# The scan's table placed between the two sums of values, and its old bank given to transposes

## The chip, the cores and the metric

The kernel runs on one core of a Trainium2 chip. The metric is the device time of one execution in microseconds (us). Three runs of the kernel before gave 1956.85, 1957.84 and 1957.93 us; the median is 1957.84 us.

A core has a matrix engine (PE; its weight loads are shown apart as PEld), a vector engine (DVE), a scalar engine (ACT), a third elementwise engine (POOL) and a queue that issues transfers (SP). Each takes its instructions in order, and semaphores order one engine's work against another's. Results of the matrix engine go to PSUM, a memory of 128 partitions with eight banks of 512 float32 values each; DVE and ACT read it there.

## The reference, cut to what matters

One decoder layer is computed on 1024 tokens of width 1024, with 16 learned meta tokens ahead of them. In order: a half-weighted SwiGLU, a normalisation and one joint projection, two groups of heads side by side (four HGRN2 heads and eight stick-breaking attention heads), an output projection, and a second SwiGLU. The change touches the stick-breaking attention alone:

```python
def block(args):
    qblk, start = args
    qpos = start + jnp.arange(BLOCK, dtype=jnp.int32)
    z = jnp.einsum('bhqd,bhkd->bhqk', qblk, k) * scale
    allowed = (kpos[None, :] < qpos[:, None]) & valid[None, :]
    log_beta = jnp.where(allowed, jax.nn.log_sigmoid(z), -jnp.inf)
    log_keep = jnp.where(allowed, jax.nn.log_sigmoid(-z), 0.0)
    suffix = lax.cumsum(log_keep, axis=3, reverse=True) - log_keep
    w = jnp.exp(log_beta + suffix)
    return jnp.einsum('bhqk,bhkd->bhqd', w, v)
```

For each block of 128 queries, every key gets a score z. Its weight is sigmoid(z) times the product of sigmoid(-z) over all later allowed keys. The values are summed with these weights.

## The kernel before, in words

**Where the stage lies.** The layer's first SwiGLU and the projections come first; the stick-breaking attention runs from about 860 to 1136 us of the span; the HGRN2 heads, the output projection and the second SwiGLU follow. On the matrix engine the order is the program's own: it is written out by hand (`manual_schedule` for the tensor engine). A planner orders the other engines' instructions and places the semaphore waits that the use of tiles asks for. It goes by the order in which the program emits the instructions: an access that has to be kept apart from an earlier one waits for the earlier one.

**Jobs.** `sb_jobs` makes 32 jobs: eight heads, each with four jobs of two neighbouring query blocks, starting at blocks 0, 6, 2 and 4. A job has three lists of steps.

- `score` (`sb_scores`): a query block's keys are cut into pieces of at most 512. The function `piece` issues two matmuls into a bank `z` (L1640, L1641), sigmoid(-z) into `keep` and sigmoid(z) into `sig` on ACT (L1642, L1643), and a running product over the reversed keys on DVE (L1646, a scan). The scan's second operand is the table `begin`, in PSUM: zeros with a reversed identity, which starts each row's product at its own diagonal. The piece with the last keys reads as many of its columns as the piece has keys (144 to 457); every other piece reads only its first column, broadcast. After a block's last piece POOL multiplies `sig` by the shifted `keep` (L1653). There are 14 pieces for a head and 112 in all.
- `turn` (`unit`, `meta`, `flip`): the matrix engine transposes the weights, up to four squares of 128 into one bank (`flip`, L1495, and L1549 for the meta tokens), and `sb_parts` takes them out as a rounded part on ACT (L1618) and a remainder on DVE (L1619), called `wu` and `wm`.
- `value` (`values`): for each block of keys two matmuls (L1570, L1572) add to the job's sum `oacc`, 128 by 256. A job has 3, 9, 5 or 7 such pairs, 24 for a head and 192 in all. After the last, `sb_out` takes the sum out on ACT (L1611) and DVE (L1612).

`braid` lays the jobs over each other: in slot n it issues the scores of job n, the transposes of job n-2 and the values of job n-3, and between them projections for the HGRN2 heads (`proj`, L249 to L251), which need neither. Within a slot the steps are sorted by their place in their list.

**The eight banks during this stage.** Two for scores (`z`), two for transposes (tag `tr`, used in turn), two for sums of values (tag `o`, used in turn), one for the projections, and one, the other projection bank, for the table `begin`. `begin` is written once, just before the braid (L2180, L2181), and only read after that.

Of the kernel before, what the change touches and what calls it, by code (L numbers as in the profile page):

```python
# [11 lines left out]
F32 = mybir.dt.float32  # L12
# [5 lines left out]
PSUM = bass.MemoryType.PSUM  # L18
DRAM = bass.MemoryType.DRAM

P = 128
# [3 lines left out]
META = 16  # L25
# [23 lines left out]
class Block:  # L49
# [1401 lines left out]
    def sb_qk(self, p, qT, kT, pool, mix, dst):  # L1451
# [31 lines left out]
        for src, c0, b0, nb in rows:  # L1483
# [5 lines left out]
                self.put_split(to, p, slice(c0, c0 + n), t[:, :n], mix, gain)  # L1489
            yield 0, 1500  # L1490

    def flip(self, src, spans):
        ps = self.ptr.tile([P, len(spans), P], F32, tag="tr", name="flip")
        for j, (s0, m) in enumerate(spans):
            self.nc.tensor.transpose(ps[:m, j, :], src[:, s0 : s0 + m], self.ident)  # L1495
        return ps

    def sb_jobs(self, keys, fetch, pool):


        nc = self.nc
        qD, kD, vD, oD = keys
        pools = pool
        heads = [(p, hh) for p in range(4) for hh in range(2)]
        kept = {}

        def load(p, hh):
            rows = slice(64 * hh, 64 * hh + 64)
            qs = fetch.tile([P, SEQ], F32R, tag="qs", name="qs", bufs=2)
            ks = [fetch.tile([P, T], F32R, tag=f"ks{i}", name="ks", bufs=2) for i in range(2)]  # L1510
            for i in range(2):
                part = slice(64 * i, 64 * i + 64)
                nc.sync.dma_start(qs.bitcast(F32)[part], qD[p, rows, i])
                for j in range(2):
                    nc.sync.dma_start(ks[j].bitcast(F32)[part], kD[p, rows, j])
            return qs, ks

        def load_v(p, hh):
            v = fetch.tile([P, 9, P], F32R, tag="v", name="v", bufs=2)
            src = vD[p, hh].rearrange("r (j a) c -> r j a c", a=4)  # L1520
            for a in range(4):
                nc.sync.dma_start(
                    v.bitcast(F32)[32 * a : 32 * a + 32],
                    src[:, :, a],
                )
            return v

        def job(p, hh, qs, ks, v, b0):
            sigs, acc, wm, wu = [], [], [], []
            score, turn, value = [], [], []  # L1530
            for bi in range(2):
                score += self.sb_scores(pool, qs, ks, b0 + bi, sigs)

            def unit(u, bi):
                if bi == 0 or b0 == 4 * u - 1:
                    wu.append([
                        pool.tile([P, 4, 256], F32R, tag=f"wu{i}", name="wu", bufs=3)
                        for i in range(2)
                    ])
                spans = [(META + P * j, P) for j in range(4 * u, min(4 * u + 4, b0 + bi + 1))]  # L1540
                ps = self.flip(sigs[bi], spans)
                self.sb_parts([t[:, : len(spans), bi * P : (bi + 1) * P] for t in wu[u]], ps)

            def meta():
                wm.extend(kept["wm"][0])
                kept["wm"].reverse()
                ps = self.ptr.tile([META, 2, P], F32, tag="tr", name="flip")
                for bi in range(2):
                    nc.tensor.transpose(ps[:, bi, :], sigs[bi][:, :META], self.ident)  # L1549
                self.sb_parts([t[:META] for t in wm], ps)  # L1550

            for bi in range(2):
                for u in range(-(-(b0 + bi + 1) // 4)):
                    n = min(4, b0 + bi + 1 - 4 * u)
                    turn.append((107 * n, lambda u=u, bi=bi: unit(u, bi)))
            turn.append((214, meta))

            def values(j):
                if j == 0:
                    acc.append(self.po.tile([P, 256], F32, tag="o", name="oacc"))  # L1560
                o = acc[0]
                if j == b0 + 2:
                    w = [t.rearrange("p b t -> p (b t)") for t in wm]
                    vj, c = v[:, 0], slice(0, 256)
                else:
                    c = slice(128, 256) if j == b0 + 1 else slice(0, 256)
                    w = [t[:, j % 4, c] for t in wu[j // 4]]
                    vj = v[:, 1 + j]
                end = j == b0 + 2
                nc.tensor.matmul(o[:, c], vj, w[0], start=j == 0, stop=False,  # L1570
                                 skip_group_check=True)
                nc.tensor.matmul(o[:64, c], vj[:, :64], w[1], start=False, stop=end,  # L1572
                                 skip_group_check=True)
                if end:
                    self.sb_out(p, hh, b0, o, kept, pool, oD)

            for j in range(b0 + 3):
                value.append((240, lambda j=j: values(j)))
            return score, turn, value

        kept["wm"] = [[fetch.tile([P, 2, P], F32R, name=f"wm{j}{i}") for i in range(2)]
                      for j in range(2)]
        for t in chain(*kept["wm"]):
            nc.vector.memset(t.bitcast(F32), 0.0)
        none = kept["wm"][1][1].rearrange("p b t -> p (b t)").bitcast(F32)[META:]
        for p in range(4):
            for a in range(4):
                to = vD[p, :, 0 if a else META :, a].rearrange("h r c -> r h c")
                nc.sync.dma_start(
                    to, none[: to.shape[0]].rearrange("r (h c) -> r h c", h=2)  # L1590
                )
        ahead, v = load(*heads[0]), load_v(0, 0)
        yield None
        pool = pools[0]
        for i, (p, hh) in enumerate(heads):
            qs, ks = ahead
            if i:
                v = load_v(p, hh)
            for b0 in (0, 6, 2, 4):
                if b0 == 2 and i + 1 < len(heads):  # L1600
                    ahead = load(*heads[i + 1])
                yield job(p, hh, qs, ks, v, b0)
# [171 lines left out]
    def run(self):  # L1774
# [21 lines left out]
        with ExitStack() as c0:  # L1796
            with ExitStack() as c1:
# [8 lines left out]
                with tc.manual_schedule(engines={nc.tensor.engine}), ExitStack() as c2:  # L1806
# [88 lines left out]
                    begin, finish = self.meta_in(marks)  # L1895
# [247 lines left out]
                def after_early():  # L2143
                    pe_ctx.close()
                    self.pz = self.pool("pz", 2, PSUM, c1)
                    self.ptr = self.pool("ptr", 2, PSUM, c1)
                    self.po = self.pool("po", 2, PSUM, c1)

                self.after_early = after_early
                columns = self.hgrn_fill(xh, xl, pst, hgD)  # L2150
# [16 lines left out]
                with tc.manual_schedule(engines={nc.tensor.engine}):  # L2167
# [7 lines left out]
                    with ExitStack() as c2:  # L2175
                        self.att.append(self.pool("att1", ctx=c2))
                        tag = self.proj_tags[0]
                        self.proj_tags = [self.proj_tags[1]] * 2
                        self.begin = self.pproj.tile([P, 512], F32, tag=tag, name="begin", bufs=1)
                        nc.vector.memset(self.begin, 0.0)  # L2180
                        nc.vector.tensor_copy(self.begin[:, 1 : P + 1], self.ident[:, ::-1])  # L2181
                        self.braid(jobs, islice(columns, 76), 1.22, 2.0, 3.0)
                    cf.close()
                    self.proj_tags[0] = tag
                    hg_ctx = ExitStack()
                    hg = self.pool("hg", ctx=hg_ctx, side="right")
# [205 lines left out]
```

## Time and profile before

| what | value |
| --- | --- |
| median of three runs | 1957.84 us |
| the profiled execution's own time | 1959.65 us |
| its span, first to last instruction | 1957.9 us |
| granted matrix clock, mean | 0.999 |
| matrix engine busy in the span | 1919.8 us (98%) |
| vector engine busy | 1390.4 us (71%) |
| scalar engine busy | 849.6 us (43%) |

A busy time is the union of an engine's instructions. The ends of matmuls are modelled, and neighbouring ones overlap in the records, so their spacing tells more than their length. Each row of a timeline gives the start, the length, the engine, the line and the tiles written and read; a bracket gives the idle time of the engine ahead of it and what ended it.

### The profile page before, as it was taken

The numbers are of one execution on the slowest core, as the hardware profiler recorded it, in microseconds if no ns is written. First come the engines' busy times: TensorE is split into PE (matmuls) and PEld (weight loads), VectorE is DVE, ScalarE is ACT, GpSimd is POOL, SyncE is SP. The second block draws the span as 40 slices with busy tenths as digits, with TensorE's granted clock in tenths as the row PEclk, the third lists the DMA queues.
The fourth block names the chain that finished last, engine by engine and source line by source line (L and its number), as shares of the span: only waits on it lengthen the run. The fifth ranks groups of instructions, "written<-read, shape, count | busy, mean of one in ns | idle before, by whom it ended". The sixth has DMA issues, their size and how long they took to land.

```text
span 1957.9 us, 30218 instructions
## 1 busy us (share of the span) xinstructions
PE 1919.8 (98%) x10607; PEld 1616.6 (83%) x10607; DVE 1390.4 (71%) x2184; ACT 849.6 (43%) x1711; POOL 450.5 (23%) x625
## 2 busy tenths in 40 slices
PE   7999999999999999999999999999999999999999
PEld 6888888788888888888898978887888888888887
DVE  7977877877678665467777766677567767766774
ACT  6523443334444544356666635433232332344443
POOL 3010100001000003133333332210544645530000
PEclk9999999999999999999999999999999999999999
DMA  7356887758965315865454177655634444469473
GB/s 213 93 165 170 253 272 243 233 203 291 375 221 188 127 54 144 193 170 148 128 148 121 57 253 225 161 208 183 198 115 140 128 131 121 132 243 318 154 231 113
DMA packets 381687, 355.54 MB, mean 182 GB/s; under 512 B 129040, under 2 KB 284560, under 8 KB 381536
## 3 DMA queue, kind: packets, MB, share of 16 engines
q1 hardware_dynamic: 359728, 288.98, 48.7%
q0 software_dynamic: 20768, 64.63, 9.5%
q8 instruction: 84, 1.38, 0.3%
q14 instruction: 67, 0.55, 0.1%
q10 hardware_dynamic: 1040, 0.00, 0.0%
HBM read 237.95 MB, written 115.57 MB: 181 GB/s over the span
## 4 chain that ended last, share of the span: by engine, by line
PE 89%; DVE 4%; DMA 3%; ACT 2%; issue 1%; POOL 1%; SPq 1%; DVEq 0%; ACTq 0%; POOLq 0%
PE o L732 21%; PE qb L450 18%; PE qa L450 12%; PE qc L450 12%; PE proj L249 5%; PE proj L251 4%; PE proj L250 4%; PE flip L1495 2%; PE wo L250 1%; PE wo L249 1%; PE wo L251 1%; PE mq L1001 1%; PE oacc L1572 1%; PE oacc L1570 1%; DMA oT<-oD 1%
## 5 line engine op out<-in xcount | busy, mean ns | idle before, releaser
L450 PE MATMUL qb<-T,wh 128*128 128x512 f32 x1056 | 344.6, 390 | 1.3 <-ACT T L309 0.8
L450 PEld LDWEIGHTS qb<-T,wh 128*128 128x128 f32 x1056 | 198.1, 188 | 46.4 <-issue 2.5
L450 PE MATMUL qa<-B,wh 128*128 128x512 f32 x696 | 226.7, 390 | 0.3 <-ACT B L835 0.2
L249 PE MATMUL proj<-xh,wh 128*128 128x512 f32 (+2 forms) x640 | 213.2, 333 | 2.6 <-ACT st L1142 1.3
L732 PE MATMUL o<-t,w 128*128 128x512 f32 x924 | 211.8, 390 | 0.7 <-DVE u L543 0.7
L251 PE MATMUL proj<-xl,wh 128*128 128x512 f32 (+2 forms) x640 | 210.2, 328 | 0.8 <-DVE xl L1957 0.8
L250 PE MATMUL proj<-xh,wl 128*128 128x512 f32 (+2 forms) x640 | 210.1, 328 | 0.0
L732 PE MATMUL o<-parts 128*128 128x512 f32 x924 | 209.6, 389 | 0.0
L450 PE MATMUL qb<-T,wl 128*128 128x512 f32 x528 | 205.5, 389 | 0.0
L732 PEld LDWEIGHTS o<-t,w 128*128 128x128 f32 x924 | 172.8, 188 | 37.8 <-ACT sgm L981 1.1
L732 PEld LDWEIGHTS o<-parts 128*128 128x128 f32 x924 | 173.5, 188 | 36.0
L362 DVE TENSOR_TENSOR wl<-s,wh 128x512 fp32r<-128x512 f32 x160 | 165.6, 1035 | 50.8 <-ACT wh L360 49.9
L360 ACT CAST wh<-s 128x512 fp32r<-128x512 f32 x160 | 99.2, 622 | 188.5 <-PE qb L450 141.1
L450 PEld LDWEIGHTS qa<-B,wh 128*128 128x128 f32 x696 | 130.5, 188 | 28.0 <-DVE B L836 0.5
L360 ACT CAST wh<-raw 128x512 fp32r<-128x512 f32 x120 | 74.4, 621 | 155.8 <-PE qc L450 111.4
L450 PE MATMUL qa<-B,wl 128*128 128x512 f32 x348 | 135.4, 389 | 0.0
L249 PEld LDWEIGHTS proj<-xh,wh 128*128 128x128 f32 x640 | 120.8, 189 | 15.0 <-ACT st L1142 2.2
L251 PEld LDWEIGHTS proj<-xl,wh 128*128 128x128 f32 x640 | 120.7, 189 | 12.3 <-DVE xl L1957 1.2
L250 PEld LDWEIGHTS proj<-xh,wl 128*128 128x128 f32 x640 | 120.8, 189 | 10.1
L450 PE MATMUL qc<-B,wh 128*128 128x512 f32 x352 | 115.1, 390 | 2.3 <-DVE u L543 2.3
L450 PE MATMUL qc<-T,wh 128*128 128x512 f32 x352 | 117.0, 394 | 0.0
L450 PEld LDWEIGHTS qb<-T,wl 128*128 128x128 f32 x528 | 99.1, 188 | 20.2
(393 smaller groups left out, 3819.4 us busy)
## 6 DMA issues: line engine op xcount, KB each, us to landing
raw<-in_ffn_w_in_dram SPq DMA_DIRECT2D x176, 256.0 KB, 4.0
raw<-in_ffn_w_out_dram SPq DMA_DIRECT2D x112, 256.0 KB, 4.5
w2in<-both SPq DMA_DIRECT2D x28, 512.0 KB, 3.4
raw<-in_w_in_dram SPq DMA_DIRECT2D x25, 512.0 KB, 5.2
ks<-kD SPq DMA_DIRECT2D x32, 260.0 KB, 4.8
wout<-both SPq DMA_DIRECT2D x16, 512.0 KB, 3.7
wh<-w2in SPq DMA_DIRECT2D x27, 256.0 KB, 3.1
wl<-w2in SPq DMA_DIRECT2D x27, 256.0 KB, 3.1
```

The costliest lines, as they stand in the source:

```text
L249: nc.tensor.matmul(ps, wh[:, s], xs, start=k == 0, stop=False)
L250: nc.tensor.matmul(ps, wl[:, s], xs, start=False, stop=False)
L251: nc.tensor.matmul(ps, wh[:, s], xl[:, k, c0 : c0 + n], start=False, stop=k == nk - 1)
L360: nc.scalar.copy(hi, src)
L362: self.block_lo = nc.vector.tensor_sub(lo, src, hi.bitcast(F32))
L450: nc.tensor.matmul(ps, a[:, k, :], b[:, k, :], start=start and k == 0 and i == 0, stop=k == 3 and i == 2, skip_group_check=True,)
L732: nc.tensor.matmul(banks[bank][m], y[:, m * P : (m + 1) * P], z, start=start and at == 0 and e == 0, stop=q == nq - 1 and e == 2, skip_gro ...
L1001: nc.tensor.matmul(ps[at : at + 32, :], self.xm[:, 4 * h + k, :], got[i, h][:, k, :], start=h == 0 and k == 0, stop=h == 1 and k == 3, til ...
L1495: self.nc.tensor.transpose(ps[:m, j, :], src[:, s0 : s0 + m], self.ident)
L1570: nc.tensor.matmul(o[:, c], vj, w[0], start=j == 0, stop=False, skip_group_check=True)
L1572: nc.tensor.matmul(o[:64, c], vj[:, :64], w[1], start=False, stop=end, skip_group_check=True)
```

## The change

The two sums and the table become one tile of 1024 columns, which is two banks. The first sum is columns 0 to 255 (the first half of the first bank), the second sum columns 768 to 1023 (the second half of the second bank), and the table columns 256 to 767: its first 256 columns in the first sum's bank, its other 256 in the second sum's. Jobs take the two sums in turn, so those starting at blocks 0 and 2 sum in the first bank, and those at 6 and 4 in the second. The bank that held the table, `tag`, is used by every third transpose: `turn_bank` hands it out once in three calls, and the two banks of tag `tr` in turn otherwise. The pool `po` of the later stages is made after the braid. No instruction is added or taken out.

```diff
+    def turn_bank(self, shape):
+
+        self.turned_in = (self.turned_in + 1) % 3
+        if self.spare and not self.turned_in:
+            return self.pproj.tile(shape, F32, tag=self.spare, name="flip", bufs=1)
+        return self.ptr.tile(shape, F32, tag="tr", name="flip")
+
     def flip(self, src, spans):
-        ps = self.ptr.tile([P, len(spans), P], F32, tag="tr", name="flip")
+        ps = self.turn_bank([P, len(spans), P])
...
             def meta():
                 wm.extend(kept["wm"][0])
                 kept["wm"].reverse()
-                ps = self.ptr.tile([META, 2, P], F32, tag="tr", name="flip")
+                ps = self.turn_bank([META, 2, P])
...
             def values(j):
                 if j == 0:
-                    acc.append(self.po.tile([P, 256], F32, tag="o", name="oacc"))
+                    acc.append(self.sums[0])
+                    self.sums.reverse()
...
                     self.ptr = self.pool("ptr", 2, PSUM, c1)
-                    self.po = self.pool("po", 2, PSUM, c1)
...
-                        self.begin = self.pproj.tile([P, 512], F32, tag=tag, name="begin", bufs=1)
+                        both = self.pool("po", 1, PSUM, c2).tile([P, 1024], F32, name="oacc")
+                        self.sums = [both[:, :256], both[:, 768:]]
+                        self.begin = both[:, 256:768]
+                        self.spare, self.turned_in = tag, 0
                         nc.vector.memset(self.begin, 0.0)
                         nc.vector.tensor_copy(self.begin[:, 1 : P + 1], self.ident[:, ::-1])
                         self.braid(jobs, islice(columns, 76), 1.22, 2.0, 3.0)
                     cf.close()
+                    self.spare = None
+                    self.po = self.pool("po", 2, PSUM, c1)
                     self.proj_tags[0] = tag
```

## The prediction

> **What bounds the kernel now.** I read the page's head first, then the table by stretch, for the stage from 860 to 1140 us in which the changed banks are used.
>
> ```profile
> span 1957.9 us, 30218 instructions
> PE 1919.8 (98%) x10607; PEld 1616.6 (83%) x10607; DVE 1390.4 (71%) x2184; ACT 849.6 (43%) x1711; POOL 450.5 (23%) x625
> ...
> 860.00:1140.00 280.00, 270.99 (x1865) 244.43 (x1864) 205.11 (x356) 181.21 (x464) 98.86 (x141) 0.99 0.44 124
> ```
>
> The columns of the last row are the stretch and its length, then busy time and count of PE, weight loads, DVE, ACT and POOL. PE is busy 270.99 of 280 us, so at most 9.0 us can be gained here, while a wait put into PE's order costs its full length: PE takes its instructions in the written order and has nothing else to do meanwhile. DVE has 75 us free and ACT 99. The waits of PE in the stage, next:
>
> ```profile
> PE flip L1495 <- DVE wu L1619: 3.6, 9, 0.8
> PE z L1640 <- ACT sig L1643: 1.9, 5, 0.5
> PE flip L1495 <- DVE wm L1619: 1.8, 3, 0.6
> ...
> PE flip L1549 <- DVE wu L1619: 0.2, 1, 0.2
> ```
>
> (Columns: total, times, longest.) Transposes wait 5.6 us in all (3.6 + 1.8 + 0.2) for a bank that DVE has not emptied. That is what a third bank can take away.
>
> **The new neighbours.** From the groups by tile:
>
> ```profile
> L1646 DVE TENSOR_TENSOR_SCAN keep<-keep,begin x112: 431/909/1160, 864.1 to 1120.4; 128x144 f32<-128x144 f32 x8, 128x272 f32<-128x272 f32 x8, 128x457 f32<-128x457 f32 x8, 128x455 f32<-128x455 f32 x8
> ...
> L1570 PE MATMUL oacc<-wu,v x160: 220/280/368, 874.0 to 1134.5; 128*128 128x256 f32 x128, 128*128 128x128 f32 x32
> ```
>
> Today the 112 scans read a bank that nobody writes. After the change each reads a bank into which PE sums values. By the layout, all 112 touch the first bank (the short read of column 0 too); those with more than 256 columns, seven pieces of a head's fourteen, also touch the second. Whether PE must then wait is the question on which all hangs. One place in the trace bears on it, where DVE reads the first of several products in one bank (columns: start, length, engine, line, tiles, idle time before):
>
> ```profile
> 1192.87 1.83 PE L1321 MATMUL up<-vr,vT 128*128 128x128 f32 x14
> ...
> 1193.18 0.68 DVE L1257 TENSOR_TENSOR KB<-KB,F 128x512 f32<-128x512 f32 x1
> ...
> 1194.07 0.73 DVE L1324 SCALAR_TENSOR_TENSOR F<-F,Ts,up 128x128 f32<-128x128 f32 x2 [0.20 <-PE up L1321]
> ```
>
> The fourteen matmuls fill two banks, eight then six, at 0.13 us each. DVE needs only the first two, done by about 1193.4, and is free at 1193.86; it still waits 0.20 us for PE, until the eighth is done (1192.87 + 8 x 0.13 = 1193.9, and the pipeline's end). So disjoint columns do not part two engines in this program: the wait covers the bank or the tile. A sum and the table within one bank will be kept apart the same way.
>
> [...]
>
> **Which side waits, and for how long.** Order goes by emission. `piece` emits two z matmuls, two ACT passes and the scan in one go. A values step placed after it must therefore wait for that scan, although PE reaches it within a fraction of a microsecond. A scan's wait for earlier sums is free: PE has passed them before it reaches this piece's z. For `sb_out` the last values step has already waited. A usual place, from the timeline:
>
> ```profile
> 877.59 0.31 PE L1641 MATMUL z<-ks,qs 128*128 128x328 f32 x1
> ...
> 877.74 0.22 PE L1570 MATMUL oacc<-wu,v 128*128 128x128 f32 x1
> ...
> 878.01 0.45 ACT L1642 ACTIVATE keep<-z 128x328 f32<-128x328 f32 x1
> ...
> 878.62 0.89 DVE L1646 TENSOR_TENSOR_SCAN keep<-keep,begin 128x327 f32<-128x327 f32 x1
> ```
>
> The sum's matmul starts 0.15 us after z's second; the scan ends at 879.51. It would be 1.77 us late. Behind it on PE stand the next transposes, z and projections; ACT's `keep` and `wu` passes and DVE's remainders wait for those, so nothing overtakes.
>
> I went so through all 192 value pairs, by job (even jobs first bank, odd jobs second), each against the last scan emitted before it that touches its bank, counting each scan once. 64 pairs come too early. The first and the last:
>
> ```profile
> 873.50 0.32 PE L1641 MATMUL z<-ks,qs 128*128 128x328 f32 x1
> ...
> 874.01 0.36 PE L1570 MATMUL oacc<-wu,v 128*128 128x256 f32 x1
> ...
> 874.20 1.47 DVE L1646 TENSOR_TENSOR_SCAN keep<-keep,begin 128x263 f32<-128x263 f32 x2
> ...
> 1116.30 0.34 PE L1641 MATMUL z<-ks,qs 128*128 128x392 f32 x1
> ...
> 1116.83 0.36 PE L1570 MATMUL oacc<-wm,v 128*128 128x256 f32 x1
> ...
> 1117.54 0.96 DVE L1646 TENSOR_TENSOR_SCAN keep<-keep,begin 128x393 f32<-128x393 f32 x1
> ```
>
> They are 875.67 - 874.01 = 1.66 and 1118.50 - 1116.83 = 1.67 us late. All 64 add up to 109 us: 96 for 46 pairs that follow their piece within 0.55 us, 13 for 18 pairs with projections between. This is the upper bound, since it has today's queues on ACT and DVE. Those get shorter when PE pauses. The lower bound takes for each size the fastest way seen from z to the scan's end:
>
> ```profile
> L1642 ACT ACTIVATE keep<-z 128x264 f32<-128x264 f32 x16 | 6.2, 386 | 4.6 <-PE z L1641 4.6
> ...
> L1642 ACT ACTIVATE keep<-z 128x456 f32<-128x456 f32 x16 | 8.9, 556 | 1.4 <-PE z L1641 0.9
> ...
> L1646 DVE TENSOR_TENSOR_SCAN keep<-keep,begin 128x455 f32<-128x455 f32 x8 | 9.2, 1154 | 0.9 <-ACT keep L1642 0.8
> ...
> L1646 DVE TENSOR_TENSOR_SCAN keep<-keep,begin 128x265 f32<-128x265 f32 x8 | 5.6, 701 | 3.4 <-ACT keep L1642 3.4
> ```
>
> For 264 keys that is 0.28 (z) + 0.39 + 0.70 and two hand-overs of 0.1, or 1.58 us; for 456 it is 0.37 + 0.56 + 1.15 and 0.07, or 2.15. Summed over the 64 it is 84 us. I take **92**, nearer the lower bound, as ACT and DVE will be only about half busy.
>
> **What comes with the waits.** A hand-over from DVE to PE costs time once more:
>
> ```profile
> 901.42 0.39 DVE L1619 TENSOR_TENSOR wm<-flip,wm 16x256 fp32r<-16x256 f32 x1
> ...
> 901.95 0.41 PE L1495 MATMUL flip<-ident,sig 128*128 128x128 f32 x2 [0.58 <-DVE wm L1619]
> ```
>
> DVE ends at 901.81, PE starts 0.14 us later. 64 of them are 0 (if hidden in the weight load) to 9 us; I take **5**. Then the granted clock, from stretches cut at its one drop within the stage (after the length stand the five engines' busy times, then the clock):
>
> ```profile
> 850.21:853.63 3.42, 2.11 (x18) 1.90 (x16) 2.30 (x4) 3.28 (x6) 1.26 (x5) 1.00 0.98 336
> ...
> 863.87:867.28 3.41, 2.39 (x11) 1.46 (x11) 3.17 (x5) 3.14 (x9) 1.30 (x4) 1.00 0.83 230
> 867.28:870.69 3.41, 3.41 (x11) 2.73 (x10) 3.20 (x6) 1.46 (x5) 2.12 (x3) 0.50 1.01 205
> ...
> 869.38 0.63 PE L250 MATMUL proj<-xh,wl 128*128 128x512 f32 x1
> 869.81 0.63 PE L251 MATMUL proj<-xl,wh 128*128 128x512 f32 x1
> ...
> 871.14 0.39 PE L249 MATMUL proj<-xh,wh 128*128 128x512 f32 x1
> 871.37 0.40 PE L250 MATMUL proj<-xh,wl 128*128 128x512 f32 x1
> ```
>
> After a stretch of 3.41 us in which PE paused for 1.0 us, the clock was halved for the next 3.41 us: matmuls of 512 columns came every 0.43 us in place of 0.23. Another stretch with 1.3 us of pause had no such sequel; it has 18 matmuls against 11. At 0.23 us for 512 columns (a transpose's counted twice) the columns streamed fill 41% of the stretch that led to a drop and 52% of the other. With the 64 waits spread over the stage's 1865 matmuls, 11 to 16 stretches (lower bound of the waits) or 19 to 27 (upper) fall under 41 to 47%. A drop costs at most 8 x 0.20 = 1.6 us, less where the stretch also holds waits; say 14 drops at 1.2, rounded to **16** us; bounds 0 and 43.
>
> [...]
>
> **The gain.** The 5.6 us of transpose waits and most of the z waits vanish, since DVE and ACT catch up in every pause: **-7** (bounds 0 and -9, all the idle time of the stage).
>
> **At nothing.** The table is set up where it was, once:
>
> ```profile
> 863.20 0.48 DVE L2180 MEMSET begin<- 128x512 f32 x1
> 863.23 0.48 PE L1640 MATMUL z<-ks,qs 128*128 128x456 f32 x1 [0.33 <-ACT sig L1643]
> ```
>
> PE waits for ACT there, not for the table; an earlier start is worth between 0 and about 1 us. A scan that reads across two banks has no row; the nearest, 457 columns in 1.10 us within one bank, gives 2.4 ns a column and DVE has 75 us free, so 0 with +1 at most. No transfer is issued elsewhere. The pool made after the braid waits for the last `sb_out`, as its banks do today: 0.
>
> **Sum** against the profiled execution's 1959.65 us: 92 + 5 + 16 - 7 = +106, or 2065.7; it lay 1.8 above the median, so **2064 us**. All low ends give 84 - 9 = +75, all high ends 109 + 9 + 43 = +161.
>
> **Rivals.** [...] *Waits by tile, not by bank*: the row at 1194.07 fits both, as its tile is one bank. Then every scan holds up every sum: 92 pairs, 120 to 163 us late; 131 + 7 + 22 - 8 = +152, or 2110 us. *Only the first bank binds*: if long scans are not counted into the second bank, 46 pairs, 57 to 77 us late; 62 + 4 + 10 - 6 = +70, or 2028 us. *The change does only what its words say*: columns do part the engines, no value waits for a scan, and the third bank takes away up to 5.6 us of transpose waits; about 4 gained, 1954 us. This ends on the other side, and decides if the values' rows keep starting 0.15 us after z. Against it speaks the 0.20 us wait at 1194.07, which columns alone would not explain.
>
> **How the numbers follow.** Chances: the forecast 0.55, waits without clock 0.15, by tile 0.08, first bank only 0.10, no waits 0.12. The range 2022 to 2102 holds the first two with their unknowns and most of the first-bank case; about 2 in 10 lie outside. Changes under 0.2% (3.9 us) can hardly be told from none. Only the last case is not slower: 0.06 faster, 0.05 the same; slower 0.89.
>
> **What would show it.** In the changed profile: PE `oacc` L1570 waiting for DVE `keep` L1646 some 64 times with a total near 92 us (right), or absent (wrong); PE's busy share in the stage down from 97% to near 75%; the stage some 105 us longer; several stretches at clock 0.5; transposes' waits for `wu` and `wm` nearly gone. A wait count near 92 would mean by tile, near 46 first bank only. The prediction falls if no value pair waits for a scan.

## The result, and the profile after

The changed kernel takes 2138.73 us at the median of five runs (2137.16 to 2146.01); before it is 1957.84 us (1956.85 to 1958.01). The ratio is 1.0931, with a 95% interval from 1.0913 to 1.0948: 9.3% slower, or 181 us. That is outside the predicted range of 2022 to 2102 us. That sums wait for scans, and that this makes the kernel slower, was as forecast. Which accesses wait for each other, and what the waits cost in clock, was not.

The head of the changed kernel's page, and the stage's row in the table by stretch (the stretch and its length, busy time and count of PE, weight loads, DVE, ACT and POOL, then the granted clock, the DMA share and GB/s):

```profile
span 2135.4 us, 30240 instructions
PE 1969.9 (92%) x10607; PEld 1644.7 (77%) x10607; DVE 1392.9 (65%) x2184; ACT 853.9 (40%) x1711; POOL 449.4 (21%) x625
PEclk9999999999999999989999899999999999999999
860.80:1312.50 451.70, 315.39 (x1851) 268.47 (x1850) 202.67 (x323) 184.68 (x462) 97.70 (x140) 0.92 0.27 76
```

The same row of the kernel before, from the first score to the last sum:

```profile
859.00:1135.50 276.50, 267.49 (x1851) 241.68 (x1850) 201.15 (x325) 180.43 (x462) 97.61 (x140) 0.99 0.44 124
```

The stage grew by 175.2 us, of a span that grew by 177.5; the work is the same. PE idles 136.3 us in place of 9.0, and its mean clock fell to 0.92. The waits of PE in the stage after the change (total, times, longest):

```profile
PE oacc L1578 <- DVE keep L1654: 121.8, 80, 3.1
PE oacc L1578 <- DVE ot L1620: 12.7, 9, 3.1
PE z L1648 <- ACT sig L1651: 1.4, 4, 0.5
```

(L1578 is the former L1570, L1654 the scan, L1620 the read-out of a sum.) The transposes' waits are gone, as forecast. The sums of values wait 89 times, 134.5 us: for scans, and, which no step of the prediction had, for the read-out of the other sum. Two places of the timeline show both kinds:

```profile
900.72 0.42 DVE L1620 TENSOR_TENSOR ot<-oacc,olow 64x256 f32<-64x256 f32 x1
...
901.19 0.41 PE L1578 MATMUL oacc<-wu,v 128*128 128x256 f32 x1 [1.10 <-DVE ot L1620]
...
919.34 0.32 PE L1649 MATMUL z<-ks,qs 128*128 128x348 f32 x1
...
920.44 0.93 DVE L1654 TENSOR_TENSOR_SCAN keep<-keep,oacc 128x347 f32<-128x347 f32 x1
...
921.43 0.38 PE L1578 MATMUL oacc<-wu,v 128*128 128x256 f32 x1 [1.56 <-DVE keep L1654]
```

At 901.19 a job starting at block 2 begins its sum in the first bank and waits until DVE has read the sum in the second bank. At 921.43 a job starting at block 4 begins its sum in the second bank and waits for a scan of 347 columns; that is not the piece with a block's last keys, so it reads one column of the first bank. Neither pair shares a bank; both share the tile. Sorted by layout, 26 of the 80 waits for scans, 39.9 of 121.8 us, are of this kind.

### The profile page after: what moved, and what is told of

Its sections match the earlier page's. It is cut to its first block, busy times and chain, and to the rows that moved or that the text cites. A ratio compares the mean times of both kernels' runs of the same rounds, so it can differ in the third digit from the quotient of the medians.

```text
span 2135.4 us, 30240 instructions
## 1 busy us (share of the span) xinstructions
PE 1969.9 (92%) x10607; PEld 1644.7 (77%) x10607; DVE 1392.9 (65%) x2184; ACT 853.9 (40%) x1711; POOL 449.4 (21%) x625
## 5 line engine op out<-in xcount | busy, mean ns | idle before, releaser
L249 PE MATMUL proj<-xh,wh 128*128 128x512 f32 (+2 forms) x640 | 221.2, 346 | 1.6 <-ACT st L1142 1.3
L250 PE MATMUL proj<-xh,wl 128*128 128x512 f32 (+2 forms) x640 | 218.3, 341 | 0.0
L251 PE MATMUL proj<-xl,wh 128*128 128x512 f32 (+2 forms) x640 | 217.4, 340 | 0.8 <-DVE xl L1965 0.8
L1578 PE MATMUL oacc<-wu,v 128*128 128x256 f32 (+1 forms) x160 | 54.7, 351 | 117.6 <-DVE keep L1654 104.8
L1661 POOL TENSOR_TENSOR sig<-sig,keep 128x144 f32<-128x144 f32 (+3 forms) x64 | 81.0, 1266 | 278.6 <-DVE keep L1654 263.9
L1578 PEld LDWEIGHTS oacc<-wu,v 128*128 128x128 f32 x160 | 31.8, 198 | 139.7 <-DVE keep L1654 123.9
L249 PEld LDWEIGHTS proj<-xh,wh 128*128 128x128 f32 x640 | 127.5, 199 | 13.8 <-ACT st L1142 1.5
L251 PEld LDWEIGHTS proj<-xl,wh 128*128 128x128 f32 x640 | 127.3, 199 | 13.4 <-DVE xl L1965 1.2
L250 PEld LDWEIGHTS proj<-xh,wl 128*128 128x128 f32 x640 | 127.3, 199 | 10.8
```

The costliest lines, as they stand in the source:

```text
L249: nc.tensor.matmul(ps, wh[:, s], xs, start=k == 0, stop=False)
L250: nc.tensor.matmul(ps, wl[:, s], xs, start=False, stop=False)
L251: nc.tensor.matmul(ps, wh[:, s], xl[:, k, c0 : c0 + n], start=False, stop=k == nk - 1)
L1661: nc.gpsimd.tensor_mul(sig, sig, keep[:, 1 : nk + 1])
```

## The experiments

Two theories stood against each other after the result. T: a wait covers the tile, whatever bank or columns the two accesses touch. B: it covers the bank, and the loss beyond the forecast 106 us has another cause. Besides, the third bank's own worth and the arithmetic of a wait were open. Lines of code below are those of the changed kernel.

**The table alone in a bank of the shared tile.**

```diff
-                        self.sums = [both[:, :256], both[:, 768:]]
-                        self.begin = both[:, 256:768]
+                        self.sums = [both[:, :256], both[:, 256:512]]
+                        self.begin = both[:, 512:]
```

> One tile of two banks as in the change, but both sums lie in its first bank (columns 0 to 511) and the table alone in its second (512 to 1023). Theory T (waits go by tile): nothing changes for the scans, sums still wait for DVE's scan some 80 times for about 120 us; the sums also wait for each other's read-out; 2115 to 2160 us. Rival B (waits go by bank): no sum waits for a scan; only the first matmul of a job waits for the read-out of the job before, at most 31 times at 1.4 us (12.7 us over 9 such waits in the changed kernel), and 1960 to 2005 us.

It took 2143.74 us; ratio to before 1.0947 (1.0932 to 1.0962). The waits of PE in its stage:

```profile
PE oacc L1578 <- DVE keep L1654: 121.7, 80, 3.1
PE oacc L1578 <- DVE ot L1620: 12.5, 9, 3.1
```

They are those of the changed kernel, to 0.2 us, although no scan touches a bank with a sum. B falls.

**The sums in one tile, the table apart again, transposes in two banks.**

```diff
                         self.sums = [both[:, :256], both[:, 768:]]
-                        self.begin = both[:, 256:768]
-                        self.spare, self.turned_in = tag, 0
+                        self.begin = self.pproj.tile([P, 512], F32, tag=tag, name="begin", bufs=1)
+                        self.spare, self.turned_in = None, 0
```

> The table is back in a bank and tile of its own and transposes have two banks as before; only the two sums are one tile of two banks. Theory T (by tile): no wait for scans, but the first matmul of a job waits for the read-out of the job before although it lies in the other bank: 9 to 31 times at about 1.4 us, 1968 to 2005 us. Rival B (by bank): the sums are free of each other, no such wait, 1955 to 1961 us.

It took 1996.35 us; ratio 1.0195 (1.0179 to 1.0210).

```profile
PE oacc L1578 <- DVE ot L1620: 34.8, 30, 3.1
```

Thirty of the 31 changes of job wait, across banks, 1.16 us each. T holds a second time. In the changed kernel only nine such waits are left because of the 31 first sums of a job that wait there, 22 wait for a scan instead (33.4 us in all).

**The change without its third bank.**

```diff
-                        self.spare, self.turned_in = tag, 0
+                        self.spare, self.turned_in = None, 0
```

> The change with the transposes left in two banks; the bank that held the table is empty during the stage. Both theories of the waits: they stay, about 134 us in all. If the third bank is worth the transposes' waits of before, at most 5.6 us, it is 2138 to 2146 us; since DVE catches up in every pause I expect 2136 to 2142 and hardly any wait of a transpose. Rival: the third bank itself costs something (a changed order on DVE or ACT), then more than 5 us faster than the changed kernel.

It took 2142.52 us (2140.11 to 2149.60), ratio 1.0947 (1.0929 to 1.0965); the changed kernel's interval, 1.0913 to 1.0948, overlaps it. The waits are 120.6 us for scans and 12.5 for read-outs, and no transpose waits. So while PE pauses for the tile, the third bank is worth no more than can be measured here: the pauses alone let DVE empty two banks in time.

**The table in SBUF, no tile shared, transposes in three banks.**

```diff
-                        both = self.pool("po", 1, PSUM, c2).tile([P, 1024], F32, name="oacc")
-                        self.sums = [both[:, :256], both[:, 768:]]
-                        self.begin = both[:, 256:768]
+                        po = self.pool("po", 2, PSUM, c2)
+                        self.sums = [po.tile([P, 256], F32, tag="o", name="oacc") for _ in range(2)]
+                        self.begin = self.pool("table", ctx=c2).tile([P, 464], BF16, name="begin")
```

> The table lies in SBUF as bf16 (its values are 0 and 1, so exact), the sums are two tiles of one bank each as before, and transposes have the third bank. If the waits for the shared tile are the whole loss, the loss is gone and only the third bank's worth is left: transposes' waits of 5.6 us fall, 1951 to 1957 us. Rival: the third bank is worth nothing because the next wait (z for ACT's sig) takes over: 1957 to 1959 us. Rival: a scan with its table in SBUF is slower than 909 ns median and DVE turns late: above 1960 us.

It took 1953.87 us against 1957.88 us for the kernel before on the same chip: ratio 0.9978 (0.9968 to 0.9988). The whole loss is gone with the shared tile, and the kernel is 4 us faster than before. The largest waits left in its stage, 858.9 to 1128.4 us:

```profile
PE z L1648 <- ACT sig L1651: 1.4, 4, 0.5
PE proj L249 <- ACT st L1135: 1.0, 3, 0.6
PE oacc L1580 <- DVE wu L1627: 1.0, 3, 0.6
```

No transpose waits. A price shows elsewhere, at the scans; by form, the kernel before and then this one (columns: count, busy time, mean ns, idle before):

```profile
L1646 DVE TENSOR_TENSOR_SCAN keep<-keep,begin 128x327 f32<-128x327 f32 x8 | 7.1, 885 | 0.0
L1646 DVE TENSOR_TENSOR_SCAN keep<-keep,begin 128x345 f32<-128x345 f32 x8 | 6.9, 858 | 0.0
```

```profile
L1654 DVE TENSOR_TENSOR_SCAN keep<-keep,begin 128x345 f32<-128x345 f32 x8 | 12.8, 1602 | 0.0
...
L1654 DVE TENSOR_TENSOR_SCAN keep<-keep,begin 128x327 f32<-128x327 f32 x8 | 7.1, 885 | 0.0
```

The 64 scans that read the table column by column take 78.3 us in place of 52.6 (345 columns: 1602 ns in the mean, before 858). The 48 that read one column take 47.9 in place of 45.5: most are unchanged (327 columns: 885 ns both times), but six are longer, one of 348 columns 2.23 us in place of 0.94. All 112 take 126 us in place of 98. What the long ones have in common stands in the last section.

**The same with two banks for transposes.**

```diff
-                        self.spare, self.turned_in = tag, 0
+                        self.spare, self.turned_in = None, 0
```

> As the SBUF table, but transposes keep two banks. If the third bank is what gained the 4 us there, this one is back at 1957 to 1961 us and waits 5 us or more for transposes (DVE is slower: its scans read SBUF twice); if the move of the table itself gained them, it stays at 1952 to 1955 us.

It took 1963.09 us, 2 us above the range; ratio 1.0027 (1.0017 to 1.0037). The move of the table alone costs 5 us, and the third bank brings the 9.2 us between the two kernels (1963.09 to 1953.87; they ran on two chips, where the kernel before took 1958.01 and 1957.88 us). The expectation puts DVE's slower scans down to SBUF being read twice; by the counts in the last section that alone slowed none by more than 12 ns with the third bank. With two banks the transposes wait 10.7 us (the three rows of L1502 and L1556), 5.1 more than the 5.6 before, so part of what the third bank brings here makes up for the slower scans:

```profile
PE flip L1502 <- DVE wu L1627: 8.1, 14, 1.2
PE flip L1502 <- DVE wm L1627: 1.6, 3, 0.6
PE flip L1556 <- DVE wu L1627: 1.0, 2, 0.8
```

**Both sums in one bank and tile, the table in another, transposes in three banks.**

```diff
-                        both = self.pool("po", 1, PSUM, c2).tile([P, 1024], F32, name="oacc")
-                        self.sums = [both[:, :256], both[:, 768:]]
-                        self.begin = both[:, 256:768]
+                        po = self.pool("po", 1, PSUM, c2)
+                        both = po.tile([P, 512], F32, name="oacc")
+                        self.sums = [both[:, :256], both[:, 256:]]
+                        self.begin = po.tile([P, 512], F32, name="begin")
```

> Two tiles of one bank each: both sums in the one, the table alone in the other; transposes have the third bank. No wait for scans (no shared tile). The first matmul of a job waits for the read-out of the job before, here by tile and by bank alike: some 30 waits, 35 us, as with the sums in one tile (1996.35 us), less 4 us of the third bank: 1988 to 1998 us. Rival: two sums in one physical bank cost more than two sums in one tile over two banks; then above 2000 us.

It took 1995.92 us; ratio 1.0195 (1.0181 to 1.0208).

```profile
PE oacc L1578 <- DVE ot L1620: 35.1, 30, 3.1
```

These are the waits of two sums in one tile over two banks (30 waits, 34.8 us), so the bank makes no difference to them. That the times agree too (1996.35 us there) shows less, since only this kernel has the third bank. A bank for transposes that is got by letting the sums share one costs far more than the 9.2 us it brought above.

**The change with values ahead of the scores.**

```diff
...
+            order = []
+            for x in sorted(now, key=lambda x: x[0]):
+                i = len(order)
+                if x[3] == value:
+                    while i and order[i - 1][3] in (0.0, turn):
+                        i -= 1
+                order.insert(i, x)
...
```

(Each step carries the lag of its list, by which scores, 0.0, and transposes are known.)

> The change as it is, with one more edit in the braid: a values step that would follow a piece or transposes directly is issued ahead of them, so that projections lie between a scan's emission and the next values step. Theory (a wait costs the scan's way from z, 1.6 to 2.2 us, less the distance on PE): 33 to 44 waits for scans, 10 to 31 us in all, and 10 to 30 us for read-outs; with the clock 1980 to 2020 us. Rival (each scan costs its wait wherever the sums are put): stays above 2100 us.

It took 2044.20 us, 24 us above the range; ratio 1.0440 (1.0425 to 1.0454). Half of the loss is gone, so the rival falls, but more is left than I expected:

```profile
PE oacc L1578 <- DVE keep L1654: 56.3, 44, 3.7
PE oacc L1578 <- DVE ot L1620: 7.7, 7, 2.7
```

The count of waits for scans is at the upper end of 33 to 44, their sum nearly twice my upper end; the waits for read-outs, 7.7 us, lie under the 10 to 30 expected. Each wait by itself goes by the arithmetic. One of them:

```profile
922.49 0.31 PE L1649 MATMUL z<-ks,qs 128*128 128x328 f32 x1
...
923.53 0.89 DVE L1654 TENSOR_TENSOR_SCAN keep<-keep,oacc 128x327 f32<-128x327 f32 x1
...
924.47 0.38 PE L1578 MATMUL oacc<-wm,v 128*128 128x256 f32 x1 [0.22 <-DVE keep L1654]
```

PE reached the sum 1.76 us after z; the scan ended 1.93 us after z; the wait is the difference and 0.05 us more. What I had wrong is that the edit would put projections ahead of every sum. In 23 of the 44 places the sum still comes 0.3 to 0.6 us after a z. All 23 are the first sum of a job, and they wait 43.9 us. The edit cannot reach them: it reorders the steps of one slot, a job's first sum is by then the first step of its slot, and the pieces and transposes ahead of it belong to the slot before. The other 21 wait 12.5 us together.

**The table beside the first sum alone.**

```diff
-                        both = self.pool("po", 1, PSUM, c2).tile([P, 1024], F32, name="oacc")
-                        self.sums = [both[:, :256], both[:, 768:]]
-                        self.begin = both[:, 256:768]
+                        po = self.pool("po", 1, PSUM, c2)
+                        both = po.tile([P, 512], F32, name="oacc")
+                        self.sums = [both[:, :256], po.tile([P, 256], F32, name="osep")]
+                        self.begin = both[:, 256:]
```

(The scan of a block's last keys is cut at 256 columns, and the rest is a second scan with the first column broadcast. That edit is not shown. L1663 below is the scan with the broadcast column.)

> The table is 256 columns and shares a tile of one bank with the first sum alone; the second sum has a tile of its own; scans over 256 columns are two instructions, the second going on with the broadcast first column (56 scans more on DVE, some 10 us of its time). This is the prediction's rival with one bank binding: 46 waits for scans, 57 to 77 us, no wait for read-outs of the other sum. By the prediction's terms 2028 us; with the price per us of wait as the change showed it (178 us slower for 134 us of waits) 1958 + 67 x 1.32, about 2046 us; range 2020 to 2065.

It took 2054.07 us; ratio 1.0493 (1.0479 to 1.0507).

```profile
PE oacc L1578 <- DVE keep L1663: 70.4, 42, 4.2
```

42 waits of 70.4 us, where 46 of 57 to 77 were expected; no read-out is waited for. The table and the first sum lie in different columns of one bank and tile here, and still wait. The prediction's way of counting comes close once it is told what waits for what. Its price for these waits, +70 us, is not: the kernel is 96 us slower.

**Where the time goes, over all runs.** For each profile I took the stage from the first z to the last sum, PE's idle time in it, and the time that the clock stood at half. A half clock loses at most half of its time: in the kernel before, at 0.50, matmuls of 512 columns came every 0.43 us in place of 0.23. The remainder is what the stage grew by, less added idle time, less half of the added time at half clock.

| kernel | stage, us | PE idle | at half clock | waits of sums | remainder |
| --- | --- | --- | --- | --- | --- |
| before | 276.5 | 9.0 | 3.4 | 2 | |
| the change | 451.7 | 136.3 | 75.1 | 89 | 12.0 |
| table alone in its bank | 456.7 | 136.0 | 88.7 | 89 | 10.6 |
| sums in one tile | 312.5 | 37.5 | 10.2 | 30 | 4.1 |
| no third bank | 464.7 | 134.9 | 112.6 | 88 | 7.7 |
| table in SBUF | 269.5 | 5.0 | 0.0 | 4 | -1.3 |
| the same, two banks | 280.3 | 13.3 | 0.0 | 2 | 1.3 |
| sums in one bank | 310.6 | 37.7 | 6.8 | 30 | 3.7 |
| values ahead | 360.7 | 67.1 | 37.5 | 51 | 9.0 |
| first sum only | 374.0 | 72.4 | 75.1 | 43 | -1.8 |

For the change: 175.2 = 127.3 of added idle time + 35.9 of clock + 12.0, and 12.0 over 89 waits is 0.13 us for each restart of PE. With the first sum only the remainder is slightly negative, because half the time at half clock is an upper bound: part of it was idle. If only the time is halved in which PE was busy at half clock (67.2 of the change's 75.1 us), the change's clock term is 31.9 and its remainder 16.1, and in the six kernels with 30 waits or more besides it the remainder is 0.09 to 0.18 us a wait. That the remainder is the restarts is read from this fit; no row shows a restart by itself.

The clock term differs from one execution to the next. The changed kernel and the one without the third bank wait alike (134.5 and 133.1 us) and stand 75.1 and 112.6 us at half clock. The profile of the change is that of its fastest execution, with a granted clock of 0.982; the other four have 0.975 to 0.980.

## Why the prediction was right or wrong

**Right: that the sums would have to wait for the scans, and that this outweighs the third bank.** It gave 0.88 to the cases with waits, and the sign followed. The kernel with the table in SBUF shows the other half: without a shared tile the loss is gone (1953.87 us against 1957.88).

**Wrong: "all 112 touch the first bank ... those with more than 256 columns ... also touch the second", as the rule for who waits.** This step counted 64 waits by bank. The row at 1194.07 us, on which it stood, fits a wait by bank and a wait by tile alike, as the prediction itself said among its rivals; it still gave the tile 0.08. The table moved to a bank of its own within the tile keeps all 80 waits for scans; the sums in two banks of one tile wait for each other 30 times. The rival's rule was the right one: every scan holds up every sum. Its count of 92 waits for scans stands against 80 found, and its 131 us against 121.8. That the totals come closer, 89 waits and 134.5 us, is luck: they hold nine waits for read-outs, which the rival did not have.

**Wrong: "For `sb_out` the last values step has already waited."** That looked at the scans alone. With both sums in one tile, the next job's first sum waits for the read-out of the job before: 9 times and 12.7 us in the changed kernel, 30 times and 34.8 us where nothing else hides it.

**Mis-sized: the clock, 16 us.** The changed kernel spent 75.1 us of the stage at half clock, at most 35.9 us more lost than before. That pauses shorter than a stretch of 3.4 us cost clock was right: the longest wait is 3.1 us, and the clock dropped 17 times from full. A stretch that was followed by half clock (0.50 in the second row) and one that was not, each 3.4 us, in the changed kernel:

```profile
887.80:891.20 3.40, 1.25 (x9) 1.10 (x9) 3.10 (x5) 1.80 (x5) 2.41 (x1) 1.00 1.05 312
891.20:894.60 3.40, 3.28 (x11) 2.89 (x12) 0.07 (x1) 0.00 (x0) 0.93 (x4) 0.50 1.03 217
956.00:959.40 3.40, 1.86 (x16) 1.65 (x15) 1.31 (x2) 1.24 (x3) 0.77 (x2) 1.00 0.60 136
959.40:962.80 3.40, 2.24 (x18) 1.94 (x17) 0.83 (x2) 1.40 (x4) 0.20 (x1) 1.00 0.13 43
```

By the prediction's count of columns at 0.23 us for 512 (a transpose's count twice, as its 128 come every 0.11 us), the first is 27% full and the third 45%. So counted from the recorded starts of the matmuls, the 17 stretches at full clock that led to a drop are 21 to 41% full. Of the 94 that led to none, five are 36 to 41% full and the rest 43% or more. Under 36%, then, each was followed by a drop, above 43% none was, and between them both happened. The bound was put at 41 to 47%. There were 22 stretches at half clock against the 14 taken, and each cost up to 1.7 us against 1.2. Too few waits explain only part of it: for the rival's 131 us of waits the prediction's own price gave 22 us, still short of 36. No run shows the low end of 0 for this term, nor the case of waits without a loss of clock, to which the prediction gave 0.15: the seven kernels with 30 waits of sums or more stood 6.8 to 112.6 us at half clock, the kernel before 3.4.

**Mis-sized: the hand-over, 5 us.** If the remainders are restarts, each costs 0.1 to 0.2 us, 12 to 16 us in the changed kernel. With 89 waits the prediction's 0.14 us would give 12.5. It was its choice of 5 from a range of 0 to 9, and the count of 64, that made the term small.

**Right: the gain, -7, and the price of one wait.** PE's idle time apart from the sums' waits fell from 8.5 us to 1.8. The reason given, that DVE and ACT catch up in every pause, is borne out by the kernel without the third bank, where no transpose waits either. A wait is the scan's way from z less PE's distance from z, and 0.05 us: in all 80 waits for scans of the changed kernel the sum's matmul starts 0.055 to 0.057 us after the scan's end.

**The sum.** The forecast was +106, and the profile's span grew by 177.5. Waits less gain were 127.3 us against 85, the clock up to 35.9 against 16, the hand-overs 12.0 or more against 5; another 2.3 us lie outside the stage and were not followed. By the rival's rule, with its +152, most of the shortfall was the clock (36 against 22).

**Open.** Why a stretch that is 36 to 41% full is followed by a drop in one place and not in another, and what the remainder is made of. No run puts two tiles into one bank, so whether a wait would then go by the bank is not shown either.

## What to carry to other kernels

A free half of a bank is not free if the planner tracks a tile: before two uses are put into one tile, list each pair of accesses on different engines and the distance between them in the order of emission, since each pair can become a wait (here 80 for scans and 9 for read-outs). The price of such a wait on a full engine (PE was busy 98% of the span) was the other engine's way minus that distance (1.93 less 1.76 us, and 0.05, in the place shown), a restart (some 0.1 to 0.2 us, an estimate from the remainders) and, where pauses left the matrix engine 21 to 41% full for 3.4 us, a clock at half speed for the next 3.4 (17 times in the changed kernel, and not after five stretches that were 36 to 41% full). The bank itself was worth having: the same third bank brought 9 us when the table moved out of PSUM, 5 of which the move cost. When steps are moved apart to hide a wait, look at the seams too: a reordering within one slot left the first sum of a slot right behind the scores of the slot before.

## What the runs showed that was not expected

With the table in SBUF, a scan and a POOL multiplication that ran together held each other up. Two places with the same pair of shapes, 100 us apart:

```profile
899.99 3.06 POOL L1661 TENSOR_TENSOR sig<-sig,keep 128x1040 f32<-128x1040 f32 x1 [3.53 <-ACT sig L1651]
900.25 0.97 DVE L1654 TENSOR_TENSOR_SCAN keep<-keep,begin 128x400 f32<-128x400 f32 x1
...
999.93 2.03 POOL L1661 TENSOR_TENSOR sig<-sig,keep 128x1040 f32<-128x1040 f32 x1 [3.53 <-PE flip L1502]
1000.19 2.62 DVE L1654 TENSOR_TENSOR_SCAN keep<-keep,begin 128x400 f32<-128x400 f32 x1
```

Once POOL takes 3.06 us and the scan its usual 0.97, once POOL takes its usual 2.03 and the scan 2.62. (In the kernel before, the eight multiplications of this size took 2.03 to 2.04 us each, the eight scans 0.97 to 0.98.) Over all 112 scans of this kernel it looks so: 56 run with no POOL multiplication, addition or subtraction beside them, and none is over 12 ns longer than its size's mean before. Of the 47 that begin while POOL is at work, 39 are 74 ns to 1.66 us longer. Of the 9 during which POOL begins, none is over 20 ns longer. In the kernel before, with the table in PSUM, 43 scans begin while POOL is at work, and scans of one size differ by at most 40 ns. So here the table's place in SBUF did not make a scan slow by itself; it did together with POOL's work, and scans with one broadcast column were hit too (6 of the 39).

What the two engines contend for is not shown. By these counts the earlier start mostly wins (39 of 47 scans slowed when POOL was ahead, none of 9 when the scan was), but POOL starts 0.26 us ahead in both places above and is held up in one of them. Starts on POOL are rough in the profile, so what decides so close a case stays open.
